# Another opening for layer 1 of a two-layer decoder trunk: transposed x, sums over features, and other placements

## The chip, the core and the metric

The kernel runs on one core of one Trainium2 chip. The metric is the device time of one execution in microseconds; the median of several runs counts. The profile is one execution recorded by the hardware profiler. TensorE multiplies, VectorE and ScalarE do the elementwise work, GpSimd (POOL) little, and SyncE (SP) issues nearly all DMAs.

## What is computed

Two layers on x (512 tokens x 2048 features, float32). Each layer normalises x, modulates it by a conditioning vector c, mixes tokens and adds the gated result:

```python
c_act = jax.nn.silu(c)
for i in range(2):
    mod = (c_act @ ada_w[i] + ada_b[i])[:, None, :]
    shift, scale, gate = jnp.split(mod, 3, axis=-1)
    h = rmsnorm(x, norm_g[i]) * (1.0 + scale) + shift
    y = retention_branch(h, ...) if i == 0 else mla_branch(h, ...)
    x = x + gate * y
return rmsnorm(x, final_norm_g)
```

`retention_branch` begins with `proj = h @ w_in`, where `w_in` holds the columns of q, k, v and a gate g for eight heads. The change concerns only what comes before and beside the first head's part of that product.

## The kernel before, in words

All work on h is done transposed: features on the 128 partitions, the 512 tokens along the free axis. The 2048 features are 16 blocks `kt` of 128, and two blocks make a pair `u` (8 pairs). For each block the kernel needs hT[kt] = a * xT + b, where xT is x transposed and multiplied by each token's 1/rms, and the columns a and b come from the conditioning. Matrices are split into a high part (float32r) and a low part (the rest), and every product is three matmuls: high by high and the two mixed ones.

The conditioning columns are dot products of rows of `ada_w`, transposed on the host (`ada_t`), with silu(c). `load_mod` loads 128 such rows (`aw`, 1 MiB, four buffers; in halves of 512 KB for blocks 0 and 1), and `sum_mod` forms the sums on VectorE with one SCALAR_TENSOR_TENSOR that multiplies and adds up, for a whole block or per half. After the second half a VectorE add joins both. `make_shift` and `make_first` (ScalarE) turn the sums into b_col and a_col; `make_first` also writes the high part of hT and a full copy `hf`, from which VectorE makes the low part.

The opening before, in order. SP loads x as eight half tiles of 512 KB (four token tiles of 128 x 2048 in two halves), then the first `aw`, then weights and more `aw` in turn. c (one row) is spread over all partitions by four one-row float32 matmuls (c_ps), and ScalarE takes the silu. Per token tile `square` sums the squares along the free axis, one half tile on ScalarE and the other on VectorE; GpSimd raises the mean to the power -1/2. `diagonal` puts the factor on a 128x128 diagonal, and `transpose` multiplies blocks of x by it on TensorE, which transposes and normalises at once. This is done for blocks 0 to 5; ScalarE copies them from PSUM to SBUF (`keep_x`). The matmuls x_r spread the factors over all partitions; `factors` is their copy. For pairs u = 3 to 7 the host's transposed x (`x_t`) is loaded later, in `load_unit`, and `normalise(u)` multiplies it by the factors on VectorE.

Then come the products of the first head: v and g of block 0, v and g of block 1, qk of blocks 0 and 1, and from there pair by pair (`products`, 12 matmuls of 512 columns for one block and one kind, four PSUM banks; `swap` changes banks between v and qk). `prepare_ahead(u)` holds the weight casts, the sums, `normalise` and `make_first` of pair u in the written order. Several things set the order around the change: every instruction wrapped in `queued` is issued behind the last one written so far for ScalarE, VectorE, TensorE and SP, so each engine works in the order of the text; SP issues loads in that order, and a load whose buffer is still in use holds up those behind it. PSUM has four `acc` and four `aux` banks.

Of the kernel before, what the change touches and what calls it, by code (L numbers as in the profile page):

```python
# [49 lines left out]
def hybrid_trunk_kernel(  # L50
# [44 lines left out]
    def big(name, dt=F32R):  # L95
        return base.tile([P, 2, T], dt, tag="big", bufs=16, name=name)
# [16 lines left out]
    def small(name, n=1):  # L113
        return base.tile([P, n], F32, tag="small", bufs=24, name=name)
# [267 lines left out]
    def sum_mod(kt, s, half=None):  # L382

        aw, n = mods[kt, s], 1 if half is None else 2
        if half != 1:
            mod_halves[kt, s] = small(f"mc_{kt}_{s}", n)
        col, j = mod_halves[kt, s], half or 0
        cols = slice(j * D // n, (j + 1) * D // n)
        DVE.scalar_tensor_tensor(  # L389
            out=aw[:, cols], in0=aw[:, cols], scalar=1.0, in1=c_all[:, cols], op0=ALU.mult, op1=ALU.mult,  # L390
            accum_out=col[:, j : j + 1],
        )
        if half == 1:
            both = small(f"mc_{kt}_{s}b")
            DVE.tensor_add(both, col[:, 0:1], col[:, 1:2])
            col = both
        if half != 0:
            mods[kt, s] = col

    def make_shift(kt):  # L400
        k1 = slice(kt, kt + 1)
        ACT.activation(b_col[0][:, k1], mods[kt, 0], AF.Identity, bias=bias_c[0][:, k1])

    def make_first(kt):

        k1 = slice(kt, kt + 1)
        if kt > 0:
            queued(make_shift, kt)
        queued(
            lambda: ACT.activation(  # L410
                a_col[0][:, k1], mods[kt, 1], AF.Identity, bias=bias1[:, k1], scale=norm_c[0][:, k1]
            )
        )
        dst, src = big(f"hT_{kt}"), xT[kt // 2][:, kt % 2, :]
# [94 lines left out]
        return f[:, 0:2, :], f[:, 2:4, :]  # L509


    xs = [[big(f"x_{t}_{j}", F32) for j in range(2)] for t in range(NT)]
    for t in range(NT):
        for j in range(2):
            nc.sync.dma_start(
                xs[t][j], x[t * P : (t + 1) * P, j * 1024 : (j + 1) * 1024].rearrange("p (a b) -> p a b", a=2)
            )
    prepares = {}

    def load_first(kind, u):  # L520
# [2 lines left out]
    def load_mods(kt):  # L523
        for s in range(2):
            mods[kt, s] = queued(load_mod, kt, s)

    load_first("v", 0)
    load_mods(0)
    queued(prepares["v", 0].load, 0)
    load_first("g", 0)  # L530
    prepares["g", 0].load(0)
    load_mods(1)
    for kind in "vg":
        queued(prepares[kind, 0].load, 1)
    load_first("qk", 0)


    c_all = l0p.tile([P, D], F32, name="c_all")
    queued(ACT.dma_start, c_all[0:1, :], c)
    queued(ACT.dma_start, rt, rot_c)  # L540
    queued(ACT.activation, small("silu_first"), ones[:, 0:1], AF.Silu)
    c_ps = [acc(f"c_ps{j}") for j in range(4)]
    for j, ps in enumerate(c_ps):
        queued(PE.matmul, ps, ones[0:1, :], c_all[0:1, j * T : (j + 1) * T], True, True)

    def silu(j):
        ACT.activation(c_all[:, j * T : (j + 1) * T], c_ps[j], AF.Silu)

    bias1 = l0p.tile([P, KD], F32, name="bias1")

    ss = [small(f"x_ss_{t}", 2) for t in range(NT)]
    norm = [None] * NT

    def square(t):
        ACT.activation(k4b(f"x_sq_{t}_0", F32), xs[t][0], AF.Square, accum_out=ss[t][:, 0:1])
        DVE.scalar_tensor_tensor(
            out=k4b(f"x_sq_{t}_1", F32), in0=xs[t][1], scalar=1.0, in1=xs[t][1], op0=ALU.mult, op1=ALU.mult,
            accum_out=ss[t][:, 1:2],
        )
        s1 = small(f"x_s1_{t}")  # L560
        DVE.tensor_add(s1, ss[t][:, 0:1], ss[t][:, 1:2])
        norm[t] = rsqrt(s1, 1, 1.0 / D, f"x_{t}")

    diags = []

    def diagonal(t):
        diags.append(l0p.tile([P, P], F32, tag="diag", bufs=4, name=f"x_diag{t}"))
        if t == NT - 1:
            ACT.activation(diags[t], ident, AF.Identity, scale=norm[t])
        else:  # L570
            DVE.tensor_scalar(out=diags[t], in0=ident, scalar1=norm[t], scalar2=None, op0=ALU.mult)
# [4 lines left out]
    xT = [k4(f"xT_{u}", F32) for u in range(NU)]  # L576
    xT_ps = []

    def transpose(t):

        if t == 0:
            xT_ps.extend(aux(f"xT_ps_{kt}") for kt in range(4))
        for kt in range(4):
            queued(
                PE.matmul, xT_ps[kt][:, t * P : (t + 1) * P],
                xs[t][0][:, kt // 4, (kt % 4) * P : (kt % 4 + 1) * P], diags[t], True, True,
            )

    for t in range(NT):
        queued(square, t)
        queued(silu, t)
        if t == 0:
            queued(
                lambda: DVE.scalar_tensor_tensor(
                    out=bias1, in0=bias_c[0][:, KD:], scalar=1.0, in1=norm_c[0], op0=ALU.add, op1=ALU.mult
                )
            )
        else:  # L600
            queued(diagonal, t - 1)
            transpose(t - 1)
    POOL.dma_start(c_d, c_all[0:1, :])
    queued(sum_mod, 0, 0, 0)
    queued(diagonal, NT - 1)
    transpose(NT - 1)

    def keep_x(kt, ps):
        queued(ACT.copy, xT[kt // 2][:, kt % 2, :], ps)

    for kt in range(3):
        keep_x(kt, xT_ps[kt])
    x_r = aux("x_r")
    for t in range(NT):
        queued(PE.matmul, x_r[:, t * P : (t + 1) * P], ones, diags[t], True, True)
    factors = tmp("x_factors")


    more_ps = [aux(f"xT_ps_{kt}") for kt in (4, 5)]
    for t in range(NT):  # L620
        for kt, ps in zip((4, 5), more_ps):
            queued(
                PE.matmul, ps[:, t * P : (t + 1) * P], xs[t][0][:, kt // 4, (kt % 4) * P : (kt % 4 + 1) * P], diags[t],
                True, True,
            )

    def normalise(u):
        DVE.tensor_mul(xT[u], xT[u], factors.unsqueeze(1).to_broadcast([P, 2, T]))
# [1 line left out]
    def load_unit(u):  # L630
        here, there = ("v", "qk") if u % 2 == 0 else ("qk", "v")
        if u > 1:
            load_first(here, u)
        load_mods(2 * u)
        if u == 1:
            load_first(here, u)
        if u > 2:
            queued(nc.sync.dma_start, xT[u], x_t[u])
# [14 lines left out]
    def prepare_ahead(u, first=None, between=lambda: None):  # L653
# [6 lines left out]
        queued(sum_mod, 2 * u, 0)  # L660
        if first is not None and u > 2:
            queued(first)
        if u > 2:
            queued(normalise, u)
        queued(low)
        queued(sum_mod, 2 * u, 1)
# [45 lines left out]
    queued(low)  # L712
    queued(low_qk)
    queued(sum_mod, 2, 0, 0)
    queued(products, "v", 1)
    queued(products, "g", 1)
    queued(swap, "v", "qk")
# [13 lines left out]
    for u in range(1, NU):  # L731
# [1884 lines left out]
```

## Time and profile before

| | |
|---|---|
| time, median of 3 runs | 2119.43 us (2119.42 to 2119.93) |
| profiled execution, first to last instruction | 2118.4 us |
| TensorE busy | 2104.0 us (99%) |
| VectorE, ScalarE, GpSimd busy | 1676.0, 1055.5, 103.6 us |
| DMA | 462.95 MB, 219 GB/s in the mean |

Times in the rows below are microseconds from the first instruction, unless ns is written. A matmul of float32 operands appears as two passes (two MATMUL records); one of float32r operands as a single one. PE is TensorE's matmul side, PEld its loading of weights.

### The profile page before, as it was taken

How to read it: one execution, taken by the hardware profiler on the slowest of the kernel's cores; microseconds unless marked ns; L12 is line 12 of the kernel's file. 1: busy time of each engine (PE TensorE's matmuls, PEld its weight loads, DVE VectorE, ACT ScalarE, POOL GpSimd, SP SyncE). 2: the span in 40 equal slices, each digit the busy share in tenths (PEclk: the TensorE clock that was granted, in tenths of full speed). 3: DMA queues.
4: the chain of work that ended last, by engine and by line, in shares of the span. 5: the costliest groups of instructions: out<-in, count | busy, mean ns of one | idle time of the engine just before them, and what ended most of it. 6: DMA issues, size and time to landing. Idle time of an engine off the chain costs nothing.

```text
span 2118.4 us, 30062 instructions
## 1 busy us (share of the span) xinstructions
PE 2104.0 (99%) x11124; PEld 1812.6 (86%) x11124; DVE 1676.0 (79%) x2506; ACT 1055.5 (50%) x1622; POOL 103.6 (5%) x176
## 2 busy tenths in 40 slices
PE   8999999999999999999999999999999999999998
PEld 6888898989889888888888888898889989888888
DVE  7899888888888789666777778768978788886665
ACT  6765444444454444434344444345446575664443
POOL 1001010000000000000000000010001000000000
PEclk9999999999999999999999999999999999999999
DMA  9975786868787778856657556753566644346643
GB/s 381 406 280 195 248 276 222 283 211 272 239 263 250 242 229 283 265 172 196 222 173 241 201 198 230 258 191 108 164 189 209 190 129 149 118 137 219 222 142 138
DMA packets 230101, 462.95 MB, mean 219 GB/s; under 512 B 20881, under 2 KB 84401, under 8 KB 226369
## 3 DMA queue, kind: packets, MB, share of 16 engines
q1 hardware_dynamic: 217312, 421.07, 60.3%
q0 software_dynamic: 11920, 38.91, 4.7%
q8 instruction: 87, 1.43, 0.3%
q10 hardware_dynamic: 722, 1.06, 0.2%
q14 instruction: 60, 0.49, 0.1%
HBM read 417.96 MB, written 43.00 MB: 218 GB/s over the span
## 4 chain that ended last, share of the span: by engine, by line
PE 96%; DMA 1%; DVE 1%; ACT 0%; issue 0%; SPq 0%; DVEq 0%
PE o L1486 16%; PE o L2450 4%; PE x L884 2%; PE x L883 2%; PE x L885 2%; PE y L885 2%; PE y L884 2%; PE s L885 2%; PE s L884 2%; PE s L883 2%; PE y L883 2%; PE uv L2046 2%; PE qk L158 2%; PE s_qk L984 2%; PE x_qk L984 2%; PE qk L160 2%
## 5 line engine op out<-in xcount | busy, mean ns | idle before, releaser
L1486 PE MATMUL o<-o_h,o_p 128*128 128x512 f32 (+1 forms) x1088 | 323.0, 378 | 0.0
L1486 PEld LDWEIGHTS o<-o_h,o_p 128*128 128x128 f32 x1088 | 200.2, 188 | 37.1
L1486 PE MATMUL o<-o_l,o_p 128*128 128x512 f32 (+1 forms) x544 | 204.8, 376 | 0.0
L136 DVE TENSOR_TENSOR o_p<-o_r,o_p 128x1024 fp32r<-128x1024 f32 x64 | 78.1, 1222 | 54.3 <-ACT o_p L135 54.1
L1486 PEld LDWEIGHTS o<-o_l,o_p 128*128 128x128 f32 x544 | 102.3, 188 | 18.3
L2450 PE MATMUL o<-o_h,o_w 128*128 128x512 f32 (+1 forms) x336 | 82.7, 337 | 0.0
L1170 DVE SCALAR_TENSOR_TENSOR mod<-mod,c_odd 128x1024 f32<-128x1024 f32 x56 | 67.2, 1219 | 15.3 <-DMA mod<-in_ada_t_dram 15.3
L135 ACT CAST o_p<-o_r 128x1024 fp32r<-128x1024 f32 x64 | 66.7, 1054 | 22.4 <-PE o L1486 13.3
L158 PE MATMUL qk<-hT,qk_p 128*128 128x512 f32 x192 | 75.0, 391 | 0.0
L160 PE MATMUL qk<-hT,qk_p 128*128 128x512 f32 x192 | 74.9, 390 | 0.0
L389 DVE SCALAR_TENSOR_TENSOR aw<-aw,c_all 128x2048 f32<-128x2048 f32 (+1 forms) x37 | 73.2, 1997 | 2.1 <-DMA aw<-in_ada_t_dram 2.1
L159 PE MATMUL qk<-hT,qk_p 128*128 128x512 f32 x192 | 74.7, 389 | 0.0
L2450 PEld LDWEIGHTS o<-o_h,o_w 128*128 128x128 f32 x336 | 57.7, 188 | 6.9
L2450 PE MATMUL o<-o_l,o_w 128*128 128x512 f32 (+1 forms) x168 | 56.5, 337 | 0.0
L136 DVE TENSOR_TENSOR o_l<-o_in,o_h 128x1024 fp32r<-128x1024 f32 x24 | 29.3, 1222 | 34.2 <-ACT o_h L135 34.2
L1332 ACT ACTIVATE yn<-y,nmr,gn_r 128x512 f32<-128x512 f32 x32 | 22.3, 778 | 67.7 <-DVE nmr L1326 67.7
L135 ACT CAST o_h<-o_in 128x1024 fp32r<-128x1024 f32 x24 | 25.3, 1052 | 61.6 <-PE o L159 40.5
L158 PE MATMUL o<-o_h,o_w 128*128 128x512 f32 x128 | 50.1, 391 | 0.0
L160 PE MATMUL o<-o_h,o_w 128*128 128x512 f32 x128 | 49.8, 389 | 0.0
L159 PE MATMUL o<-o_l,o_w 128*128 128x512 f32 x128 | 49.8, 389 | 0.0
L1170 DVE SCALAR_TENSOR_TENSOR mod<-mod,c_bm 128x1024 f32<-128x1024 f32 x40 | 48.7, 1219 | 0.0
L448 PE MATMUL g<-hT,g_p 128*128 128x512 f32 x192 | 46.1, 389 | 0.0
(1532 smaller groups left out, 6238.3 us busy)
## 6 DMA issues: line engine op xcount, KB each, us to landing
mod<-in_ada_t_dram SPq DMA_DIRECT2D x96, 512.0 KB, 5.7
o_r<-in_ret_w_out_dram SPq DMA_DIRECT2D x64, 512.0 KB, 5.5
aw<-in_ada_t_dram SPq DMA_DIRECT2D x28, 1024.0 KB, 9.5
mod_gate<-in_ada_t_dram SPq DMA_DIRECT2D x32, 512.0 KB, 4.4
o_w_raw<-in_mla_w_out_dram SPq DMA_DIRECT2D x32, 512.0 KB, 4.4
qk_r<-in_ret_w_in_dram SPq DMA_DIRECT2D x48, 256.0 KB, 3.5
qk_r<-qk_d SPq DMA_DIRECT2D x32, 256.0 KB, 6.1
v_r<-v_d SPq DMA_DIRECT2D x32, 256.0 KB, 5.7
```

The lines of the kernel that those rows point to most:

```text
L135: ACT.copy(hi, src)
L136: DVE.tensor_sub(lo, src, hi.bitcast(F32))
L158: PE.matmul(o, lhs[0], rhs[0], start=first and not seeded, stop=False, skip_group_check=seeded)
L159: PE.matmul(o, lhs[0], rhs[1], start=False, stop=False, skip_group_check=seeded)
L160: return PE.matmul(o, lhs[1], rhs[0], start=False, stop=last, skip_group_check=seeded)
L883: PE.matmul(banks[b], a[0], w[0], start=first, stop=False, skip_group_check=True)
L884: PE.matmul(banks[b], a[0], w[1], start=False, stop=False, skip_group_check=True)
L885: PE.matmul(banks[b], a[1], w[0], start=False, stop=True, skip_group_check=True)
L984: PE.matmul(o, w[wp][:, i, b * P : (b + 1) * P], a[ap], start=first and i + b + k == 0, stop=k == 2, skip_group_check=True,)
L1170: DVE.scalar_tensor_tensor(out=aw, in0=aw, scalar=1.0, in1=silu_c[j], op0=ALU.mult, op1=ALU.mult, accum_out=row_sums[piece][:, j, b : b + 1],)
L1486: PE.matmul(o, w[i][:, ki, c0 + b * P : c0 + (b + 1) * P], a[j], start=first and i + j == 0, stop=last and i == 1, skip_group_check=True,)
L2450: PE.matmul(banks2[b][:, cols], w[0][i][:, 0, b * P : (b + 1) * P], o2_moving(w, u, cols)[j], start=u + i + j == 0, stop=u == KD - 1 and i ...
```

## The change

In words: the x read at the start is now mostly the host's transposed x. SP loads pairs 2 to 7 of `x_t` first (six times 512 KB), then the first half of `aw` for block 0, then the first 512 features of the four token tiles (four times 256 KB), then `vecs` (bias and gain columns, before on GpSimd's queue), then the rest in turn. Pairs 0 and 1 are still transposed on TensorE, all four token tiles in one place, and x_r with them. The squares of pairs 2 to 7 are formed on ScalarE and added up elementwise on VectorE (`square_pair`); TensorE sums them over the partitions (`x_sums`), and the squares of the first 512 features are summed on ScalarE as before (`square`, `norm_pair`). The diagonals are all made on ScalarE. The row c is split into a high and a low float32r part (`row_parts`) and spread by eight one-row matmuls (`row_spread`). Six matmuls whose result nobody reads (`keep_busy`) are put between. hT_0 is formed straight from PSUM and in two halves, and ScalarE copies the factors before a_col. The two half sums are joined on ScalarE: the first half goes into the bias (`half_shift`, `half_scale`), the second is added to it. Pair 2 is normalised on VectorE like the later ones, the loads of `x_t` leave `load_unit`, and the load of `rot` and the store `c_d` move.

```diff
-    POOL.dma_start(vcol, vecs)
...
-        if half == 1:
-            both = small(f"mc_{kt}_{s}b")
-            DVE.tensor_add(both, col[:, 0:1], col[:, 1:2])
-            col = both
         if half != 0:
-            mods[kt, s] = col
+            mods[kt, s] = col[:, n - 1 : n]
+
+    def half_shift(kt):
+        k1 = slice(kt, kt + 1)
+        ACT.activation(b_col[0][:, k1], mod_halves[kt, 0][:, 0:1], AF.Identity, bias=bias_c[0][:, k1])
+
+    def half_scale(kt):
+        k1 = slice(kt, kt + 1)
+        ACT.activation(
+            bias1[:, k1], mod_halves[kt, 1][:, 0:1], AF.Identity, bias=bias1[:, k1], scale=norm_c[0][:, k1]
+        )
...
-        dst, src = big(f"hT_{kt}"), xT[kt // 2][:, kt % 2, :]
+        dst, src = big(f"hT_{kt}"), xT[kt // 2][:, kt % 2, :] if kt > 0 else xT_ps[0]
-        n = 2 if kt == 1 else 1
+        n = 2 if kt < 2 else 1
...
+    queued(ACT.dma_start, c_all[0:1, :], c)
+    for u in range(2, NU):
+        nc.sync.dma_start(xT[u], x_t[u])
...
+    queued(load_mod_half, 0, 0)
+    for t in range(NT):
+        nc.sync.dma_start(xs[t], x[t * P : (t + 1) * P, 0:T])
+    nc.sync.dma_start(vcol, vecs)
     load_first("v", 0)
-    load_mods(0)
+    queued(load_mod_half, 0, 1)
+    queued(load_mod_half, 1, 0)
     queued(prepares["v", 0].load, 0)
+    queued(load_mod_half, 1, 1)
...
+    def row_parts(j):
+        cols = slice(j * 1024, (j + 1) * 1024)
+        queued(ACT.copy, c_row[0][j], c_all[0:1, cols])
+        queued(DVE.tensor_sub, c_row[1][j], c_all[0:1, cols], c_row[0][j].bitcast(F32))
+
+    def row_spread(j):
+        for i in range(2):
+            queued(PE.matmul, c_ps[j], one_row, c_row[i][j // 2][:, j % 2 * T : (j % 2 + 1) * T], i == 0, i == 1)
...
+    def keep_busy(src):
+        queued(PE.matmul, early, ones, src, True, True)
...
+    def square_pair(u):
+        sq = sq_sum if u == 2 else k4b(f"x_sq_{u}", F32)
+        queued(ACT.activation, sq, xT[u], AF.Square)
+        if u == NU - 1:
+            queued(DVE.tensor_add, sq_sum[:, 0, :], sq_sum[:, 0, :], sq_sum[:, 1, :])
+            for i in range(2):
+                queued(DVE.tensor_add, sq_sum[:, 0, :], sq_sum[:, 0, :], sq[:, i, :])
+        elif u > 2:
+            queued(DVE.tensor_add, sq_sum, sq_sum, sq)
...
+    row_parts(0)
+    square_pair(2)
+    row_parts(1)
+    square_pair(3)
+    keep_busy(xT[2][:, 0, :])
+    keep_busy(xT[2][:, 1, :])
+    row_spread(0)
+    row_spread(1)
+    silu(0)
+    square_pair(4)
+    silu(1)
+    keep_busy(xT[4][:, 0, :])
+    row_spread(2)
+    row_spread(3)
+    square_pair(5)
+    silu(2)
+    square_pair(6)
+    silu(3)
+    keep_busy(xT[6][:, 0, :])
+    square_pair(7)
+    queued(sum_mod, 0, 0, 0)
+    x_sums = acc("x_sums")
+    for t in range(NT):
+        queued(PE.matmul, x_sums[:, t : t + 1], sq_sum[:, 0, t * P : (t + 1) * P], crow, True, True)
...
     for t in range(NT):
         queued(square, t)
...
+    for t in (2, 3):
+        keep_busy(xs[t])
+    norm_pair(0)
+    norm_pair(2)
...
+    for t in range(NT):
+        diagonal(t)
+        cols = slice(t * P, (t + 1) * P)
+        for kt in range(4):
+            queued(PE.matmul, xT_ps[kt][:, cols], xs[t][:, kt * P : (kt + 1) * P], diags[t], True, True)
+        queued(PE.matmul, x_r[:, cols], ones, diags[t], True, True)
...
-        if u > 2:
+        if u > 1:
             queued(normalise, u)
...
+    queued(half_shift, 0)
     queued(sum_mod, 0, 0, 1)
     queued(make_shift, 0)
+    queued(sum_mod, 0, 1, 0)
+    queued(half_scale, 0)
     low_v = queued(prepares["v", 0], 0)
-    for half in range(2):
-        queued(sum_mod, 0, 1, half)
+    queued(ACT.copy, factors, x_r)
+    queued(sum_mod, 0, 1, 1)
     low = make_first(0)
     queued(low_v)
     queued(sum_mod, 1, 0, 0)
     low_g = queued(prepares["g", 0], 0)
     queued(low)
     queued(low_g)
-    keep_x(3, xT_ps[3])
-    queued(ACT.copy, factors, x_r)
-    for i, ps in enumerate(more_ps):
-        keep_x(4 + i, ps)
+    for kt in range(1, 4):
+        keep_x(kt, xT_ps[kt])
+    queued(nc.sync.dma_start, c_d, c_all[0:1, :])
+    queued(half_shift, 1)
     queued(sum_mod, 1, 0, 1)
...
-    for half in range(2):
-        queued(sum_mod, 1, 1, half)
+    queued(sum_mod, 1, 1, 0)
+    queued(half_scale, 1)
+    queued(sum_mod, 1, 1, 1)
     lows = [queued(prepares[kind, 0], 1) for kind in "vg"]
...
+        if u == 2:
+            queued(ACT.dma_start, rt, rot_c)
```

## Rows read from the trace of the kernel before

**Rows 1.** The page: span, and busy time with its share and instructions.
```profile
span 2118.4 us, 30062 instructions
PE 2104.0 (99%) x11124; PEld 1812.6 (86%) x11124; DVE 1676.0 (79%) x2506; ACT 1055.5 (50%) x1622; POOL 103.6 (5%) x176
```
**Rows 2.** Waits of TensorE, whole span: engine, line, waited for: total us, times, longest.
```profile
PE c_ps L474 <- DMA c_all<-in_c_dram: 3.2, 1, 3.2
PE xT_ps L474 <- DVE x_diag L571: 2.2, 3, 1.2
PE v L448 <- DVE hT L423: 0.9, 1, 0.9
```
**Rows 3.** Chain of waits, first 120 us: start, duration, what ended last.
```profile
52.31 10.61 DMA aw<-in_ada_t_dram
...
63.02 2.30 DVE aw L389 x2
...
65.98 1.19 PE v L448 x4
...
69.91 8.16 PE qk L448 x36
```
**Rows 4.** Timeline of TensorE: start, duration, line, out<-in, form, passes, [idle before].
```profile
3.25 7.16 PE L474 MATMUL c_ps<-c_all,ones 1*128 1x512 f32 x8 [3.25 <-DMA c_all<-in_c_dram]
...
16.79 4.07 PE L474 MATMUL xT_ps<-x_diag,x 128*128 128x128 f32 x16 [0.48 <-DVE x_diag L571]
20.65 1.92 PE L474 MATMUL x_r<-x_diag,ones 128*128 128x128 f32 x8
22.36 2.04 PE L474 MATMUL xT_ps<-x_diag,x 128*128 128x128 f32 x16
24.16 3.00 PE L448 MATMUL v<-pair,hT 128*128 128x512 f32 x12
...
29.98 3.12 PE L448 MATMUL v<-pair,hT 128*128 128x512 f32 x12
```
**Rows 5.** Timeline of ScalarE, the same columns.
```profile
4.72 1.06 ACT L555 ACTIVATE x_sq<-x 128x1024 f32<-128x1024 f32 x1 [1.52 <-DMA x<-in_x_dram]
...
22.91 0.80 ACT L422 ACTIVATE h_0f<-xT,b_col,a_col 128x512 f32<-128x512 f32 x1
...
24.61 0.58 ACT L474 COPY x_factors<-x_r 128x512 f32<-128x512 f32 x1
...
28.90 0.39 ACT L410 ACTIVATE a_col<-mc_1b,bias,vcol 128x1 f32<-128x1 f32 x1 [0.26 <-DVE mc_1b L395]
29.32 1.10 ACT L420 ACTIVATE hT<-xT,b_col,a_col 128x256 fp32r<-128x256 f32 x2
...
55.92 1.04 ACT L361 CAST g_p<-g_raw 128x1024 fp32r<-128x1024 f32 x1
56.87 1.04 ACT L361 CAST qk_p<-qk_raw 128x1024 fp32r<-128x1024 f32 x1
```
**Rows 6.** Timeline of VectorE, the same columns.
```profile
14.85 1.23 DVE L556 SCALAR_TENSOR_TENSOR x_sq<-x 128x1024 f32<-128x1024 f32 x1 [0.68 <-DMA x<-in_x_dram]
...
23.75 0.69 DVE L423 TENSOR_TENSOR hT<-h_0f,hT 128x512 fp32r<-128x512 f32 x1
...
27.44 1.22 DVE L389 SCALAR_TENSOR_TENSOR aw<-aw,c_all 128x1024 f32<-128x1024 f32 x1
```
**Rows 7.** One line's instructions, L2483: durations min/median/max in ns, first and last start.
```profile
L2483 PE MATMUL x_sums<-ones,x_sq x8: 250/250/271, 2106.2 to 2107.3; 128*128 128x1 f32 x8
```
**Rows 8.** Windows: stretch, its length, busy by engine, granted clock, DMA share, GB/s.
```profile
6.00:7.00 1.00, 1.00 (x3) 0.48 (x2) 0.99 (x1) 0.35 (x1) 0.00 (x0) 1.00 0.99 231
...
8.00:9.00 1.00, 1.00 (x2) 0.33 (x1) 0.18 (x1) 0.52 (x1) 0.38 (x1) 1.00 1.01 414
```
**Rows 9.** Windows at the end of the span, the same columns.
```profile
2111.00:2112.00 1.00, 0.13 (x2) 0.00 (x0) 1.00 (x2) 0.67 (x1) 0.00 (x0) 1.00 1.04 381
...
2115.00:2116.00 1.00, 0.00 (x0) 0.00 (x0) 0.00 (x0) 0.00 (x0) 0.00 (x0) 0.50 1.03 258
```

More of the change, by code (lines that the diff above doesn't have):

```diff
@@ L509, in staged0 @@
         return f[:, 0:2, :], f[:, 2:4, :]
[L512 to L517, printed above, removed]
+    xT = [k4(f"xT_{u}", F32) for u in range(NU)]
+    xs = [base.tile([P, T], F32, tag="big", bufs=16, name=f"x_{t}") for t in range(NT)]
     prepares = {}
@@ L525, in load_mods, with load_mod_half @@
             mods[kt, s] = queued(load_mod, kt, s)
+    c_all = l0p.tile([P, D], F32, name="c_all")
+    c_row = [
+        [base.tile([1, 1024], F32R, tag="big", bufs=16, name=f"c_row{i}{j}") for j in range(2)] for i in range(2)
+    ]
+    queued(ACT.dma_start, c_all[0:1, :], c)
+    for u in range(2, NU):
+        nc.sync.dma_start(xT[u], x_t[u])
+    mods[0, 0], mods[0, 1] = (l0p.tile([P, D], F32, tag="aw", bufs=4, name=f"aw_0_{s}") for s in range(2))
+    def load_mod_half(s, j):
+        cols = slice(j * 1024, (j + 1) * 1024)
+        nc.sync.dma_start(mods[0, s][:, cols], ada_t[0, s * D : s * D + P, cols])
+    queued(load_mod_half, 0, 0)
+    for t in range(NT):
+        nc.sync.dma_start(xs[t], x[t * P : (t + 1) * P, 0:T])
+    nc.sync.dma_start(vcol, vecs)
     load_first("v", 0)
-    load_mods(0)
+    queued(load_mod_half, 0, 1)
+    queued(load_mod_half, 1, 0)
     queued(prepares["v", 0].load, 0)
+    queued(load_mod_half, 1, 1)
     load_first("g", 0)
-    prepares["g", 0].load(0)
+    queued(prepares["g", 0].load, 0)
     load_mods(1)
@@ L535, in hybrid_trunk_kernel @@
     load_first("qk", 0)
-    c_all = l0p.tile([P, D], F32, name="c_all")
-    queued(ACT.dma_start, c_all[0:1, :], c)
-    queued(ACT.dma_start, rt, rot_c)
     queued(ACT.activation, small("silu_first"), ones[:, 0:1], AF.Silu)
     c_ps = [acc(f"c_ps{j}") for j in range(4)]
-    for j, ps in enumerate(c_ps):
-        queued(PE.matmul, ps, ones[0:1, :], c_all[0:1, j * T : (j + 1) * T], True, True)
+    one_row = base.tile([1, P], F32R, tag="tmp", bufs=6, name="one_row")
+    DVE.tensor_copy(one_row, ones[0:1, :])
@@ L546, in silu @@
+    def row_parts(j):
+        cols = slice(j * 1024, (j + 1) * 1024)
+        queued(ACT.copy, c_row[0][j], c_all[0:1, cols])
[3 more added lines that the diff above has]
+            queued(PE.matmul, c_ps[j], one_row, c_row[i][j // 2][:, j % 2 * T : (j % 2 + 1) * T], i == 0, i == 1)
     def silu(j):
-        ACT.activation(c_all[:, j * T : (j + 1) * T], c_ps[j], AF.Silu)
+        queued(ACT.activation, c_all[:, j * T : (j + 1) * T], c_ps[j], AF.Silu)
@@ L549, in hybrid_trunk_kernel @@
     bias1 = l0p.tile([P, KD], F32, name="bias1")
-    ss = [small(f"x_ss_{t}", 2) for t in range(NT)]
-    norm = [None] * NT
-    def square(t):
[L555 to L558, printed above, removed]
-        )
-        s1 = small(f"x_s1_{t}")
-        DVE.tensor_add(s1, ss[t][:, 0:1], ss[t][:, 1:2])
-        norm[t] = rsqrt(s1, 1, 1.0 / D, f"x_{t}")
@@ L564, in hybrid_trunk_kernel @@
-    diags = []
+    early = aux("early")
+    def keep_busy(src):
+        queued(PE.matmul, early, ones, src, True, True)
+    sq_sum = k4b("x_sq_2", F32)
+    def square_pair(u):
[7 more added lines that the diff above has]
+            queued(DVE.tensor_add, sq_sum, sq_sum, sq)
@@ new lines, in hybrid_trunk_kernel, with norm_pair @@
+    ss = [small(f"x_ss_{i}", NT) for i in range(4)]
+    norm = small("x_norm", NT)
+    def square(t):
+        queued(lambda: ACT.activation(tmp(f"x_sq_{t}"), xs[t], AF.Square, accum_out=ss[0][:, t : t + 1]))
+    def norm_pair(t):
+        two = slice(t, t + 2)
+        queued(
+            lambda: DVE.scalar_tensor_tensor(
+                out=ss[2][:, two], in0=ss[0][:, two], scalar=1.0 / D, in1=ss[1][:, two], op0=ALU.mult, op1=ALU.add
+            )
+        )
+        queued(lambda: POOL.tensor_tensor(out=norm[:, two], in0=ss[2][:, two], in1=mhalf[:, 0:2], op=ALU.pow))
@@ L566, in diagonal @@
+    diags = [l0p.tile([P, P], F32, tag="diag", bufs=4, name=f"x_diag{t}") for t in range(NT)]
     def diagonal(t):
[L567 to L571, printed above, removed]
+        queued(lambda: ACT.activation(diags[t], ident, AF.Identity, scale=norm[:, t : t + 1]))
@@ L575, in hybrid_trunk_kernel @@
     tables = rotary_tables(*ret_tables, 0, False, "ret", ACT)
[L576 to L587, printed above, removed]
+    row_parts(0)
+    square_pair(2)
+    row_parts(1)
@@ L591, in hybrid_trunk_kernel @@
+    queued(
+        lambda: DVE.tensor_scalar(
+            out=ss[1], in0=x_sums[:, 0:NT], scalar1=1.0 / D, scalar2=EPS, op0=ALU.mult, op1=ALU.add
+        )
+    )
     for t in range(NT):
         queued(square, t)
[L593 to L606, printed above, removed]
+    for t in (2, 3):
+        keep_busy(xs[t])
+    norm_pair(0)
+    norm_pair(2)
+    queued(
+        lambda: DVE.scalar_tensor_tensor(
+            out=bias1, in0=bias_c[0][:, KD:], scalar=1.0, in1=norm_c[0], op0=ALU.add, op1=ALU.mult
+        )
+    )
+    x_r = acc("x_r")
+    xT_ps = [aux(f"xT_ps_{kt}") for kt in range(4)]
+    for t in range(NT):
[4 more added lines that the diff above has]
+        queued(PE.matmul, x_r[:, cols], ones, diags[t], True, True)
@@ L608, in keep_x @@
+    factors = tmp("x_factors")
     def keep_x(kt, ps):
         queued(ACT.copy, xT[kt // 2][:, kt % 2, :], ps)
[L611 to L625, printed above, removed]
@@ L636, in load_unit @@
             load_first(here, u)
-        if u > 2:
-            queued(nc.sync.dma_start, xT[u], x_t[u])
         if u > 1:
@@ L662, in prepare_ahead @@
             queued(first)
-        if u > 2:
+        if u > 1:
             queued(normalise, u)
@@ L714, in hybrid_trunk_kernel @@
     queued(sum_mod, 2, 0, 0)
+    queued(half_shift, 2)
     queued(products, "v", 1)
```

3 lines of the change are left out of this document (2 added, 1 removed).

## Prediction

> **What bounds the kernel now.** I read the page first, then who waited for whom on TensorE, then the chain of waits of the first 120 us, then the first 60 us engine by engine. TensorE is busy for 2104.0 us of a span of 2118.4 us [rows 1], so time can only come from places where it idles or multiplies nothing useful. The view of waits puts nearly all idle time into the opening: 3.2 us before the first matmul, 2.2 us between groups of transposes, and one wait of 0.9 us for the low part of hT [rows 2]. After 65.98 us TensorE runs on without a gap that counts, 36 matmuls of 512 columns in 8.16 us, 0.2267 us each [rows 3]. So the question is: **when can the matmuls at 65.98 us start after the change?** Everything behind them moves along.
>
> The chain shows what holds them. The load of `aw` for feature block 6 lands at 62.9, VectorE sums it for 2.3 us, then makes the low part of hT_5, and only then does TensorE go on [rows 3]. The first 62 us are thus partly a matter of DMA, which runs at some 410 GB/s from 8 us on [rows 8]. TensorE alone would have been there sooner: from the second feature block's products at 29.98 [rows 4] to the matmuls at 65.98 there are 152 matmuls, 34.5 us at 0.2267, which gives 64.4. So 1.5 us of the 36.0 are stalls; about 1.0 of it is the wait on that load, 0.5 are short waits for hT. If the front comes up to 1 us late, the wait for `aw` absorbs it; if it comes early, that wait grows, because the same 4 MiB of x are still loaded ahead of it.
>
> The clock: the granted clock reads 1.00 in every early row, but the pace is that of 1.2 GHz. Eight passes of c_ps took 7.16 us, 0.895 each, and sixteen of the transposes 3.86 us, 0.24 each, up to 20.65; the sixteen that start at 22.36 need 1.80 us up to the first product, 0.11 each, the pace of 2.4 GHz [rows 4]. Before it rose, TensorE had worked without a gap from 16.79 on; 7.16 us of one-row matmuls had not raised it.
>
> **The change, part by part.** *Loads.* Before the first product, x costs 4 MiB as before (six transposed pairs 3 MiB, four quarter rows 1 MiB). The 2.5 MiB saved are those of pairs 3 to 7 behind 54 us, where TensorE and not DMA is late: worth nothing. The table `rot` and `vecs` leave the start; at 6 to 7 us the DMA moved 231 GB/s against 414 at 8 to 9 us [rows 8], so up to 1 us of load time may come back, less what `vecs` costs on SP. On SP, `vecs` and later the copy `c_d` wait for nothing that is late; the moved load of `rot` costs ScalarE one DMA issue at u = 2, beside a full TensorE.
>
> *ScalarE up to the last squares.* The first pair can be there at 4.72, as the first half tile of x was [rows 5]. ScalarE then does six squares and the second row copy; such instructions of 1024 columns take 1.06 and follow each other after 0.95 [rows 5], so 6.7 us. The four silus add 0.5 each, 2.0. It also waits for TensorE, which has to do two `keep_busy` first: each is two passes of 512 columns, at 0.895 [rows 4] 3.6 us for the two, to 8.3; then one-row matmuls, and c_ps0 is ready at about 9.2, when ScalarE has been idle since 7.6. A shorter wait of this kind comes before silu 2 (0.6). Sum: 4.7 + 6.7 + 2.0 + 1.6 + 0.6 = 15.6 for the last pair square. The data are there: the last 512 KB of x landed at 14.85 [rows 6], and half a MiB of `aw` is now ahead of the quarter rows.
>
> *Sum of squares and factors.* VectorE adds as ScalarE delivers; behind the last square stand two adds of 512 columns, 0.69 each [rows 6], as long as the low part of hT, so 17.1. TensorE sums across partitions in eight passes; the one similar group took 1.35 us for eight at the high clock [rows 7], I take 1.8 at the low one: 19.0. The roots (VectorE, POOL, ScalarE) need another 2 us, to about 21.5, but TensorE does two more `keep_busy` first: 3.6 us at the low pace, to 22.6. So these hide the roots and cost 1 us on top.
>
> *Transposes.* What was spread over the time up to 24.16, tile by tile, now comes in one block: 16 transposes and 4 of x_r, 40 passes. The two ends are 0.24 and 0.11 each [rows 4], 9.4 or 4.4 us. I take the high pace: by then TensorE has worked without a gap since 17.1. So x_r is done at E = 27.0.
>
> At this place the trace has to be weighed against what the early `keep_busy` are for. TensorE's last matmul ended just after 2111 and the granted clock was at 0.50, the 1.2 GHz level, in 2115 to 2116 [rows 9]: idle time of a few us brings it back. In the opening TensorE would stand idle from about 11 or 15 us to 17.1. If the clock rises with the first tiles and holds, the sums, `keep_busy` and transposes are 3 us shorter (rival 1); I hold it likelier that it is low at 17. The Trainium skill, "TensorE: Matmul & The Clock Gate", section "HAM oscillation", says that a kernel whose bursts of matmuls are parted by waits for data falls back to the low clock and pays for the rise each time. By that rule the early `keep_busy` gain nothing and the forecast stands; without it rival 1 would.
>
> *First products.* The new order on ScalarE puts the copy of x_r (`factors`) ahead of a_col and hT_0, so hT_0 waits for the very last of the 40 passes; before it needed only block 0. From E: 0.3 to drain (estimate from the 250 ns of a one-column pass [rows 7]), `factors` 0.58, a_col 0.42 until the next begins, hT_0 in two halves 1.0, its full copy 0.80 [rows 5]: E + 3.1 = 30.1. Before, that copy ended at 23.71. TensorE's first products can start at E + 1.9, but the next block's decide: behind the full copy VectorE has, in order, the low parts of hT_0 and g and three half sums of 1.22 [rows 6], then come a_col and hT_1. That took 6.3 us before (23.71 to 29.98). The two joining adds go (0.3 less), but `half_scale` now stands on ScalarE ahead of the casts of v and g and waits for the second of these sums (0.3 more): 6.3 again. The second block's products start at 36.4 instead of 29.98: **6.4 us late**. VectorE's idle time in between, over 5 us, can't be used, as the low part of hT_0 is queued ahead of the sums.
>
> *What is given back.* The wait for `aw` at 63 us vanishes (1.0). VectorE gets one multiplication of 1024 columns (1.22 [rows 6]) at u = 2, as pair 2 now has to be normalised; it fits into 2 us of waits for loads that vanish too, and may cost 0.1 to 0.2 of TensorE. `aw` of block 3 is issued some 6 us later, as its buffers come free with those sums; its users are late by the same. So 6.4 - 0.9 = 5.5.
>
> **Rivals.** *1. The clock is up from the first tiles and holds.* Then ScalarE waits less (last square at 14.6), the sums end at 17.6, two `keep_busy` take 1.7, 40 passes 4.4: E = 23.8, 3.2 earlier. For it: two `keep_busy` are 3.6 us of full matmuls at the start. Against it: one-row matmuls behind them, which didn't raise it before, and the idle stretch ahead of the sums. 2119.4 + 2.3 = 2121.7.
>
> *2. Faster: the opening is bound by loads alone.* If hT_0's full copy came by 23.7 despite the block of passes, only the load of `aw` at 62.9 would decide, and the quieter start of the DMA would bring it about 1 us forward: 2118.4. The point is E = 20.6 for the copy, and 21.5 for no change at all; that needs the chain to the last square to be over 3 us shorter than worked out, at the high clock. Little speaks for it: the 0.95 per square and 0.11 per pass are read, not guessed. That the reading of x only moves, and saves nothing where it matters, is in this rival's and in the forecast's sum alike.
>
> *3. Later still.* The clock stays low for the 40 passes as well (E up to 31.9), or the later issue of `aw` makes DMA run dry. Each would add 3 to 5 us: 2128 to 2130.
>
> **How the numbers follow.** The sums are differences inside the profiled execution (span 2118.4), whose median run took 2119.43, 1.0 more around the span; I carry the difference over. Forecast: 2119.4 + 5.5 = 2124.9, chance 0.50, with its own spread 2123.0 to 2127.0 from where the clock rises and from ScalarE's queue. Rival 1: 0.28, at 2121.7, from 2120.8 on. Rival 2: 0.11. Rival 3: 0.11. The range 2120.8 to 2127.0 leaves out rivals 2 and 3. A difference of 0.2%, 4.2 us, is about what can be told from no change. Slower by more than that: most of the forecast (0.42), rival 3 (0.11), a little of rival 1 (0.02), 0.55. Within: 0.08 + 0.26 + 0.10 = 0.44. Faster by 4.2 us would need all of the opening's gaps: 0.01.
>
> **What would show it.** In the profile after: c_ps done past 9 us, the last pair square near 15.6, `x_sums` near 17 to 19, transposes in one block from 22.6 at 0.11 a pass, `factors` at 27.3, the second block's v products near 36, VectorE idle for some us ahead of hT_0's low part, and no gap at 66 us. Transposes done by 24 show rival 1; the first hT_0 ahead of 22 us shows rival 2. It would be wrong if ScalarE and VectorE did not run in the order written, or if the pace of the passes were another.

## The result, and the profile after

The changed kernel took 2125.64 us in the median of eight runs (2124.41 to 2126.81), the kernel before, run beside it, 2119.89 us (2118.85 to 2120.45). The ratio is 1.0026 with a 95% interval of 1.0017 to 1.0036: 5.75 us slower, where 5.5 had been forecast. The profiled execution took 2126.18 us, its span is 2124.4 us against 2118.4 before.

The page, for [rows 1]:

```profile
span 2124.4 us, 30076 instructions
PE 2106.9 (99%) x11128; PEld 1811.5 (85%) x11128; DVE 1679.5 (79%) x2496; ACT 1061.6 (50%) x1636; POOL 101.8 (5%) x172
```

TensorE's waits over the whole span, the three largest, for [rows 2] (line, waited for: total us, times, longest):

```profile
PE early L480 <- DMA xT<-in_x_t_dram: 4.6, 1, 4.6
PE v L454 <- ACT hT L426: 3.1, 2, 1.6
PE x_sums L480 <- DVE x_sq L480: 2.4, 1, 2.4
```

TensorE is busy 2.9 us longer, and its three largest waits make 10.1 us instead of 6.3: that is 6.7 us against a span 6.0 us longer. Two kinds of wait are gone, that for the diagonals and that for the low part of hT. Two new ones stand in the list: 1.6 us twice for hT on ScalarE, and 2.4 us for the squares.

The chain of waits shows where the loss ends up, at the four matmuls that were at 65.98 [rows 3]:

```profile
71.67 0.62 DVE hT L429
72.28 0.04 issue
72.33 1.19 PE v L454 x4
...
76.25 8.16 PE qk L454 x36
```

They start at 72.33, 6.35 us later. From the last pass of the opening up to them the chain holds no load any more, only work of VectorE and ScalarE (sums, casts, hT and its low parts). All of the span's 6.0 us, then, has been lost by 72 us. TensorE's timeline, for [rows 4], shows when:

```profile
4.59 3.75 PE L480 MATMUL early<-xT,ones 128*128 128x512 f32 x4 [4.59 <-DMA xT<-in_x_t_dram]
8.27 2.07 PE L480 MATMUL c_ps<-c_row,one_row 1*128 1x512 f32 x4
10.27 2.07 PE L480 MATMUL early<-xT,ones 128*128 128x512 f32 x2
...
14.27 2.08 PE L480 MATMUL early<-xT,ones 128*128 128x512 f32 x2
18.73 1.84 PE L480 MATMUL x_sums<-ones,x_sq 128*128 128x1 f32 x8 [2.38 <-DVE x_sq L480]
20.42 3.64 PE L480 MATMUL early<-x,ones 128*128 128x512 f32 x4
23.90 1.05 PE L480 MATMUL xT_ps<-x_diag,x 128*128 128x128 f32 x8
...
28.14 0.39 PE L480 MATMUL x_r<-x_diag,ones 128*128 128x128 f32 x2
30.09 3.05 PE L454 MATMUL v<-pair,hT 128*128 128x512 f32 x12 [1.56 <-ACT hT L426]
...
37.39 3.12 PE L454 MATMUL v<-pair,hT 128*128 128x512 f32 x12 [1.53 <-ACT hT L426]
```

The second block's products start at 37.39 instead of 29.98, 7.41 late; of this 1.06 comes back up to 72.33. The rest is read on ScalarE and VectorE. ScalarE, for [rows 5]: the two silus that waited, the last pair square, `factors`, and the full copy of hT_0:

```profile
9.52 0.60 ACT L480 ACTIVATE c_all<-c_ps 128x512 f32<-128x512 f32 x1 [2.10 <-PE c_ps L480]
...
13.53 0.60 ACT L480 ACTIVATE c_all<-c_ps 128x512 f32<-128x512 f32 x1 [1.03 <-PE c_ps L480]
...
15.45 1.06 ACT L480 ACTIVATE x_sq<-xT 128x1024 f32<-128x1024 f32 x1
...
28.57 0.59 ACT L480 COPY x_factors<-x_r 128x512 f32<-128x512 f32 x1 [2.52 <-PE x_r L480]
...
30.39 0.78 ACT L428 ACTIVATE h_0f<-xT_ps,b_col,a_col 128x512 f32<-128x512 f32 x1
```

VectorE, for [rows 6]: the adds of the squares, and the low part of hT_0 with the last sum behind it:

```profile
15.10 1.23 DVE L480 TENSOR_TENSOR x_sq<-x_sq,x_sq 128x1024 f32<-128x1024 f32 x1 [1.35 <-ACT x_sq L480]
16.36 0.69 DVE L480 TENSOR_TENSOR x_sq<-x_sq 128x512 f32<-128x512 f32 x1
17.16 1.42 DVE L480 TENSOR_TENSOR x_sq<-x_sq,x_sq 128x512 f32<-128x512 f32 x2
...
31.19 0.69 DVE L429 TENSOR_TENSOR hT<-h_0f,hT 128x512 fp32r<-128x512 f32 x1 [3.27 <-ACT h_0f L428]
...
34.70 1.22 DVE L388 SCALAR_TENSOR_TENSOR aw<-aw,c_all 128x1024 f32<-128x1024 f32 x1
```

VectorE stands idle for 3.27 us ahead of the low part of hT_0, with three sums of 1.22 us queued behind it that need nothing from it.

### The profile page after: what moved, and what is told of

Same layout as the page of the kernel before. It is cut to its first block, busy times and chain, and to the rows that moved or that the text cites. A ratio compares the mean times of both kernels' runs of the same rounds, so it can differ in the third digit from the quotient of the medians.

```text
span 2124.4 us, 30076 instructions
## 1 busy us (share of the span) xinstructions
PE 2106.9 (99%) x11128; PEld 1811.5 (85%) x11128; DVE 1679.5 (79%) x2496; ACT 1061.6 (50%) x1636; POOL 101.8 (5%) x172
## 3 DMA queue, kind: packets, MB, share of 16 engines
q10 hardware_dynamic: 722, 1.06, 0.2%
## 4 chain that ended last, share of the span: by engine, by line
PE 97%; DVE 1%; issue 1%; ACT 1%; DMA 0%; DVEq 0%
PE o L1534 16%; PE o L2498 4%; PE x L932 2%; PE x L933 2%; PE s L933 2%; PE y L933 2%; PE x L931 2%; PE y L932 2%; PE s L932 2%; PE y L931 2%; PE s L931 2%; PE uv L2094 2%; PE qk L158 2%; PE s_qk L1032 2%; PE x_qk L1032 2%; PE qk L160 2%
```

## Experiments

The theory: the loss is made of waits that the written order brings in. The early `keep_busy` delay the squares, `factors` delays hT_0, and hT_0's low part delays the sums of block 1. The rivals: the clock's height decides, or the loads do. Every kernel is compared with the kernel before of the same session. The runs of one kernel spread over 1.4 to 4.1 us, so parts under 1 us are read from the places of the matmuls in the profiled execution. "The end of the front" below is the start of the four matmuls of block 5 that were at 65.98 before and 72.33 after.

### The `keep_busy` matmuls

**no_early_busy**: the first four are left out (nobody reads their result).

```diff
-    keep_busy(xT[2][:, 0, :])
-    keep_busy(xT[2][:, 1, :])
...
-    keep_busy(xT[4][:, 0, :])
...
-    keep_busy(xT[6][:, 0, :])
```

> The first four keep_busy (on pairs 2, 2, 4 and 6) are left out, nothing else. Theory: they only hold up c_ps and with it ScalarE; the last pair square ends near 13.5 instead of 16.5, x_sums starts near 15 instead of 18.7, and the 40 passes still run at the high pace of 0.11, since the last two keep_busy raise the clock. x_r is then done near 24.5 instead of 28.4, the second block's v products start near 33.5 instead of 37.4, and the kernel is 2 to 3 us slower than before, not 6. Rival: the early ones are what raises the clock. Then the 40 passes take 0.24 each, x_r is done at 29 or later and the time stays at before + 6.

Measured: 2123.89 us against 2120.08, 3.8 slower than before instead of 5.75 (ratio 1.0019, 1.0009 to 1.0028), where 2 to 3 had been expected. TensorE's timeline:

```profile
15.51 1.84 PE L480 MATMUL x_sums<-ones,x_sq 128*128 128x1 f32 x8 [5.94 <-DVE x_sq L480]
17.21 3.76 PE L480 MATMUL early<-x,ones 128*128 128x512 f32 x4
20.76 1.75 PE L480 MATMUL xT_ps<-x_diag,x 128*128 128x128 f32 x8
...
22.57 1.06 PE L480 MATMUL xT_ps<-x_diag,x 128*128 128x128 f32 x8
```

The sums start 3.2 us earlier (15.51 for 18.73), because the silus no longer wait for TensorE. The sums and the late `keep_busy` have the same pace as with the early ones (1.84 and 3.76 us). Only the first transposes are slower, 1.75 for eight instead of 1.05, so x_r is done 2.5 earlier, not 3.2. Between these two executions, then, the early `keep_busy` cost 3.2 us and gave 0.7 back; the 0.7 is not sure to be theirs, as in `three`, also without them, the first eight transposes took 1.16. By the medians their net cost is 1.9.

**no_busy**: the two late ones left out as well (`keep_busy(xs[t])` for t = 2 and 3).

> All six keep_busy are left out. Theory (the clock is low unless full matmuls run without a gap just ahead): the 40 passes run at 0.24 at first, 9.4 us if it never rises, and start when the roots are ready, near 19 to 20; x_r done at 28 to 29.5, later than in no_early_busy by 4, time before + 5 to 7. Rival: keep_busy only costs time; then the 40 passes end by 24 and the time is that of before + 1 to 2.

Measured: 2124.56 us, 4.5 slower than before (1.0022, 1.0012 to 1.0031), 0.7 slower than with the late ones, which the spread of the runs doesn't tell from nothing. The transposes start at 19.07 instead of 20.76, but run at 0.23 us a pass until about 24. The second block's products are at 35.28 instead of 34.94. The expectation (5 to 7 slower than before) had the late ones worth more. They shorten the block of passes by 2.0 us (26.42 - 19.07 against 26.08 - 20.76), and they start it 1.7 later: nearly all that their clock gives they cost themselves.

### The order on ScalarE and VectorE

**factors_later**: `factors` behind the full copy of hT_0, all `keep_busy` kept.

```diff
-    queued(ACT.copy, factors, x_r)
     queued(sum_mod, 0, 1, 1)
     low = make_first(0)
+    queued(ACT.copy, factors, x_r)
```

> ScalarE copies x_r (factors) behind hT_0's full copy instead of ahead of a_col. Theory: hT_0 then waits only for block 0's last transposes; v products of block 0 start near 28.5 instead of 30.1, those of block 1 near 35.8 instead of 37.4, time 1.6 us less than the changed kernel, before + 4.2. Rival: something else, the a_col column or VectorE, holds hT_0: no change, before + 5.8.

Measured: 2124.92 us, 4.8 slower than before (1.0022, 1.0013 to 1.0032), 0.9 less than the changed kernel. From the last of the 40 passes to the second block's products it takes 7.5 us (27.78 to 35.29) instead of 8.9, so 1.4 less: hT_0 now needs block 0's transposes alone. This execution shows something else too, on TensorE's timeline and in the windows (stretch, length, busy by engine with TensorE first, granted clock, DMA share, GB/s):

```profile
7.86 1.19 PE L480 MATMUL c_ps<-c_row,one_row 1*128 1x512 f32 x4
8.98 1.12 PE L480 MATMUL early<-xT,ones 128*128 128x512 f32 x2
...
11.39 2.08 PE L480 MATMUL early<-xT,ones 128*128 128x512 f32 x2
...
18.38 3.76 PE L480 MATMUL early<-x,ones 128*128 128x512 f32 x4
```

```profile
10.00:11.00 1.00, 1.00 (x5) 0.66 (x4) 0.80 (x1) 1.00 (x3) 0.00 (x0) 0.91 1.06 434
11.00:12.00 1.00, 1.00 (x3) 0.50 (x2) 0.79 (x2) 1.00 (x3) 0.00 (x0) 0.50 0.98 399
```

Here the early `keep_busy` did raise the clock: from 8 us on a `keep_busy` of two passes takes 1.12 us instead of 2.07. At about 10.8, among the one-row matmuls and with TensorE busy throughout, the granted clock falls to 0.50, and the fourth `keep_busy`, the sums and the late ones go at the low pace again. So whether or not these four raise the clock early, it is low at 16 to 22 us in both executions.

The mean granted clock, on record for every run, shows how often this happens. It is 0.996 in this execution and 0.999 in the profiled one of the changed kernel. Of the changed kernel's eight runs four have 0.996 or 0.997 and are 4.9 us slower than before in the mean; four have 0.999 and are 6.4 slower. `factors_later` and `sums_first` have four runs of ten at 0.996 or 0.997; no kernel without the four `keep_busy` in these places has a run below 0.998. So in some two of five executions they seem to raise the clock for a while, which is worth 1.5 to 2.3 us. That the clock rose and fell in those runs as it did here is read from the mean alone. Among the runs at 0.999 and above, `no_early_busy` is 2.6 us faster than the changed kernel, `factors_later` 1.1 and `sums_first` 1.4.

**sums_first**: the four half sums of block 1 ahead of hT_0's low part on VectorE.

```diff
-    queued(sum_mod, 1, 0, 0)
+    for s_ in range(2):
+        for half in range(2):
+            queued(sum_mod, 1, s_, half)
     low_g = queued(prepares["g", 0], 0)
     queued(low)
...
-    queued(sum_mod, 1, 0, 1)
...
-    queued(sum_mod, 1, 1, 0)
...
-    queued(sum_mod, 1, 1, 1)
```

> VectorE does all four half sums of block 1 before the low part of hT_0, in the time in which it sat idle (24.6 to 26.1 and 27.9 to 31.2). Theory (the order of VectorE's queue is what delays block 1): its v products start near 36.0, bound by ScalarE then, instead of 37.4; the gap of 1.5 us on TensorE behind block 0's products nearly closes; time 1.4 us less than the changed kernel, before + 4.4. Rival: ScalarE's own queue (copies of pairs 0 and 1, casts) is the bound anyway: block 1 at 37.4, before + 5.8.

Measured: 2124.67 us, 4.6 slower than before (1.0020, 1.0010 to 1.0029), 1.2 less than the changed kernel. TensorE's timeline:

```profile
33.31 2.89 PE L454 MATMUL g<-hT,g_p 128*128 128x512 f32 x12
36.04 2.90 PE L454 MATMUL v<-pair,hT 128*128 128x512 f32 x12
```

The second block's products follow g without a gap; the second wait of 1.53 us for hT is gone. It was the order on VectorE that had made this wait.

**three**: the first four `keep_busy` out, `factors` later and the sums first, together.

> The three edits so far in one kernel: first four keep_busy left out, factors behind hT_0's full copy, the four half sums of block 1 ahead of hT_0's low part. Theory (each takes a different piece off one chain: the last square, hT_0's wait, VectorE's idle time): v products of block 0 start near 25.5 to 26, those of block 1 near 31.3 with no gap between, TensorE gapless to the end, the matmuls that stand at 72.3 in the changed kernel at 66.3 to 66.8, time before + 0.3 to + 1.0. Rival: the pieces overlap and their gains don't add up: before + 2.5 or more.

Measured: 2121.31 us against 2119.90, 1.4 slower (1.0006, 0.9997 to 1.0015). The three single gains, 1.9, 0.9 and 1.2, sum to 4.0; together they gave 4.3. The front ends at 68.0. That is still a little more than expected, because of a new wait:

```profile
29.65 1.20 PE L454 MATMUL v<-pair,hT 128*128 128x512 f32 x4 [1.15 <-DVE hT L429]
```

Now hT_0 is early, and its low part stands behind the sums that were put ahead of it.

**three_xr**: besides, the x_r passes behind all the transposes, as hT_0 and not x_r is now waited for.

> As three, and the matmuls of x_r come behind all sixteen transposes instead of one behind each token tile. Theory: they fill TensorE's wait for hT_0; block 0's products start 0.6 us earlier than in three, time before - 0.3 to + 0.4. Rival: loads of aw bound the front by then as they do before, and a wait of some tenths shows near 66 us; time as three.

Measured: 2121.08 us, 1.2 slower (1.0006, 0.9997 to 1.0015). In the profile the second block's products start at 32.47 instead of 33.42; the median moved 0.2, which the spread of the runs doesn't tell from nothing. The wait for the low part is still there (1.23 us), and the time is above what was expected.

**mid**: besides, the fourth of these sums behind the low parts.

```diff
-    for s_ in range(2):
-        for half in range(2):
-            queued(sum_mod, 1, s_, half)
+    for s_, half in ((0, 0), (0, 1), (1, 0)):
+        queued(sum_mod, 1, s_, half)
...
     queued(half_scale, 1)
+    queued(sum_mod, 1, 1, 1)
```

> As three_xr, but the last of the four half sums of block 1 stands behind the low parts of hT_0 and g. Theory: TensorE's wait of 1.2 us for the low part of hT_0 (block 0) goes down to some 0.2, block 1's products at 31.1 to 31.5 instead of 32.5, time 1.0 less than three_xr: that of before, +- 0.4. Rival: ScalarE's half_scale or a_col holds block 1: as three_xr, before + 1.2.

Measured: 2120.11 us against 2120.08 (1.0001, 0.9992 to 1.0009): the kernel before is reached. TensorE's timeline, and the chain, in which the front's four matmuls are the last of these twelve:

```profile
27.80 1.21 PE L454 MATMUL v<-pair,hT 128*128 128x512 f32 x4 [0.32 <-DVE hT L429]
...
31.60 2.88 PE L454 MATMUL v<-pair,hT 128*128 128x512 f32 x12
```

```profile
64.41 2.75 PE v L454 x12
```

The wait shrinks to 0.3, the second block's products are at 31.60, and the front ends at 66.2, against 65.98 before. As far as the runs can tell (some 2 us to either side), the whole loss is thus made good by the places of `factors`, x_r and the half sums in the written order and by leaving out four matmuls that nobody reads. The block of passes itself still ends later than the transposes did before, and more sums stand ahead of the low part than before; so part of what these edits win makes up for a loss that they did not cause.

### Whether the clock decides

**fill_only**: the changed kernel, with the four early `keep_busy` moved: on pairs 3 and 4, in one block behind the last one-row matmul, where TensorE would be idle and no silu waits for them.

```diff
-    keep_busy(xT[2][:, 0, :])
-    keep_busy(xT[2][:, 1, :])
...
-    keep_busy(xT[4][:, 0, :])
     row_spread(2)
     row_spread(3)
+    keep_busy(xT[3][:, 0, :])
+    keep_busy(xT[3][:, 1, :])
+    keep_busy(xT[4][:, 0, :])
+    keep_busy(xT[4][:, 1, :])
...
-    keep_busy(xT[6][:, 0, :])
```

> The changed kernel with the four early keep_busy moved: they stand behind the last one-row matmul (on both halves of pairs 3 and 4) and fill the time in which TensorE waits for x_sq, where they hold up nothing. Theory (the clock falls in that idle stretch, and full matmuls right up to x_sums keep it up): x_sums take about 1.0 instead of 1.8, the last two keep_busy 1.7 instead of 3.6, the 40 passes 0.11 each from the first one; the roots (near 20.5) are the bound then and x_r is done near 22.5 to 23, against 25.9 in no_early_busy; v products of block 1 near 32, time before + 1.0 to + 1.8. Rival: the clock isn't up at 15.5 after 6 us of such matmuls either; then as no_early_busy, before + 3.8.

Measured: 2121.27 us, 1.2 slower than before (1.0006, 0.9997 to 1.0015). TensorE's timeline:

```profile
9.54 6.60 PE L480 MATMUL early<-xT,ones 128*128 128x512 f32 x8
16.37 1.02 PE L480 MATMUL x_sums<-ones,x_sq 128*128 128x1 f32 x8 [0.24 <-DVE x_sq L480]
17.26 1.96 PE L480 MATMUL early<-x,ones 128*128 128x512 f32 x4
```

Here the clock is up when the squares are there: the sums take 1.02 instead of 1.84, the late ones 1.96 instead of 3.76. Against no_early_busy this is 2.6 us by the medians, and the second block's products start 2.2 earlier (32.73 for 34.94): what a clock that holds is worth. It is the same means as in the change, put where it delays nobody and isn't followed by idle time.

**filled**: mid and this block of `keep_busy` together.

> mid and fill_only in one. Theory: x_r done near 22 and hT_0 at 22.5; from there VectorE's sums and the loads of aw for block 1 (landing near 26) hold block 1, near 29.5 to 30, and the load of aw for block 6 near 63 holds the front as in the kernel before: time before - 0.8 to + 0.3, and no further gain can come from the opening. Rival: TensorE alone is the bound all the way, and the 2 to 3 us from the clock come through in full: before - 2.

Measured: 2120.62 us, 0.5 slower than before (1.0004, 0.9995 to 1.0012): no better than mid and a little above what was expected (0.8 faster to 0.3 slower), although the same block had brought 2.6 in fill_only. TensorE's timeline, a load in the chain of waits, VectorE's third sum of block 1, and two windows:

```profile
23.26 2.34 PE L454 MATMUL v<-pair,hT 128*128 128x512 f32 x8
27.29 1.90 PE L454 MATMUL v<-pair,hT 128*128 128x512 f32 x4 [1.70 <-DVE hT L429]
28.99 3.83 PE L454 MATMUL g<-hT,g_p 128*128 128x512 f32 x12
```

```profile
16.46 8.91 DMA aw<-in_ada_t_dram
```

```profile
25.40 1.23 DVE L388 SCALAR_TENSOR_TENSOR aw<-aw,c_all 128x1024 f32<-128x1024 f32 x1
```

```profile
22.00:24.00 2.00, 1.97 (x14) 1.69 (x14) 1.89 (x5) 1.74 (x4) 0.00 (x0) 1.00 1.04 414
...
25.00:30.00 5.00, 3.31 (x9) 2.29 (x10) 4.94 (x10) 4.58 (x11) 0.00 (x0) 0.75 1.07 398
```

The first products start at 23.26, 0.9 earlier than before. But hT_0's low part stands behind VectorE's third sum of block 1, and that starts only at 25.40, as its `aw` lands, right behind the second sum. VectorE's waits for loads ahead of it make 1.0 us in all, at a DMA rate of 414 GB/s; the order has its share in TensorE's wait of 1.7 us too, as this sum (1.23) stands ahead of the low part. After it TensorE is still 0.5 us ahead of mid (27.29 for 27.80). Then the clock costs more than that: it falls around the wait (0.75 in the mean of 25 to 30), and four matmuls take 1.90 for 1.21, the next 12 take 3.83 for 2.91. So the second block starts at 32.66, 1.1 later than in mid. A version with this sum elsewhere was not tried, so whether the two gains can be had together stays open. None of these kernels beats the kernel before by more than the runs can tell.

### The start of the loads

**before_quiet**: the kernel before, with `vecs` on SP behind x, `rot` at u = 2, and `bias1` formed later, as it needs `vecs`.

```diff
-    POOL.dma_start(vcol, vecs)
...
+    nc.sync.dma_start(vcol, vecs)
...
-    queued(ACT.dma_start, rt, rot_c)
...
+        if u == 2:
+            queued(ACT.dma_start, rt, rot_c)
```

> The kernel before, with only two loads moved as the change moves them: vecs goes to SP behind the x loads, rot to the pass u = 2 (the bias1 instruction stands behind the first pair of half sums, as vecs is later). Theory of rival 2 in the prediction (the quieter start of DMA brings the loads forward by up to 1 us, and the load of aw for block 6 holds the front): last x tile near 13.8 instead of 14.85, aw of block 6 about 0.8 earlier, time before - 0.6 to - 1.0. Rival: the slow stretch at 6 to 7 us is not due to these two loads: no change.

Measured: 2119.79 us against 2119.90 (1.0000, 0.9992 to 1.0009): nothing. The windows, for [rows 8]:

```profile
5.00:6.00 1.00, 1.00 (x3) 0.48 (x2) 0.13 (x1) 1.00 (x3) 0.00 (x0) 1.00 0.92 160
6.00:7.00 1.00, 1.00 (x2) 0.39 (x2) 1.00 (x1) 0.25 (x1) 0.00 (x0) 1.00 0.63 225
```

The slow stretch stays without the small loads; `before_quiet_join`, also without them, has 225 GB/s in 6 to 7 us as well. Rival 2's gain from a quiet start has fallen.

**before_quiet_join**: besides, the half sums joined on ScalarE as in the change.

> As before_quiet, and the half sums joined on ScalarE as in the change (half_shift, half_scale), nothing else of it. Theory: VectorE loses four small adds of 0.16 ahead of block 1, whose products start 0.3 to 0.6 earlier, but the load of aw for block 6 holds the front anyway: time as before_quiet, within 0.3. Rival: half_scale on ScalarE waits ahead of the casts of v and g and block 1 comes later: up to + 0.5 over before_quiet.

Measured: 2120.23 us (1.0002, 0.9993 to 1.0011). The joins can't be told from nothing, as the prediction had it: less work on VectorE, one more wait on ScalarE.

## Why the prediction was right, and where its sizes were off

**The question was the right one.** All of the loss lies ahead of 72 us; the time went with the start of the matmuls at 65.98.

**The squares on ScalarE: 15.6 forecast, 16.5 measured.** The start (4.47), the pace of 0.95 and the two `keep_busy` (3.75 for 3.6) were as worked out. The waits of the silus were 2.10 and 1.03, for 1.6 and 0.6 in the sum. Ahead of the second lies the third `keep_busy` (2.07 us), between the two halves of the row; the sum gave the 0.6 without a working and named only the first two.

**The adds on VectorE: 1.5 us forecast from the last square to the sums, 2.2 measured.** The sum counted the two adds behind the last square. But the add of pair 6 (1.23) and the fold of the two halves (0.69) end only at 17.05, 0.5 behind that square, and the two wait for them. With the first point the sums start at 18.73 instead of 17.1: this was the largest error.

**Sums, late `keep_busy`, passes.** 1.84 for 1.8, 3.64 for 3.6, 40 passes in 4.63 (23.90 to 28.53) for 4.4. The roots took longer than the 2 us taken: the two powers on GpSimd alone take 2.91 us. The late `keep_busy` hid it, as the prediction said; the last pass ended at 28.5 for 27.0. (At the low pace the 40 passes would make 9.6 us, not the 9.4 of the prediction; only rival 3 uses it.)

**The first products: E + 3.1 forecast, E + 2.6 measured; then 6.3 forecast, 6.2 measured.** The reading that the block of passes, `factors` and the fixed order of VectorE set the second block's start is what factors_later, sums_first and mid show: each place undone gives its part back. The second block is 7.4 late, for 6.4 forecast.

**Given back: 0.9 forecast, 1.06 measured.** The wait of 0.9 us for the low part of hT, which ended behind `aw` [rows 2, 3], has vanished, and TensorE is without a gap from 37.39 to the end of the front but for some 0.4 us (34.94 us for 152 matmuls, 34.5 at 0.2267).

**The total.** By places in the trace it is 6.35, by spans 6.0, by medians 5.75; the forecast of 5.5 is 0.9 below the first and 0.25 below the last. In the terms of the sum the last pass is 1.5 late, the copies 0.5 early, the return 0.2 larger: the errors cancel in part. That the median came within 0.25 is luck. It lies between two groups of runs, 4.9 and 6.4 slower than before (see `factors_later`); the sum takes the low clock up to the passes, as the profiled execution has it, and so belongs beside the 6.4.

**Rival 1**, that the clock rises early and holds, was half right: in the profiled execution of factors_later it rose, and by the mean clock in half of the changed kernel's runs, and it did not hold. In the Trainium skill's "TensorE: Matmul & The Clock Gate", section "HAM oscillation", bursts parted by waits fall back to the low clock. The trace of filled agrees: around a wait of 1.70 us the granted clock fell. The fall in factors_later is another case, as TensorE was busy in it (1.00 of 1.00 us) with one-row matmuls. fill_only shows the 2.6 us that a burst without a pause gives. **Rival 2** needed the full copy of hT_0 by 23.7; it ended at 31.17. Its gain fell with before_quiet, and filled shows what else stands against it: with hT_0 earlier than before, the loads of `aw` for block 1 come in beside the order of the sums. Of **rival 3**, one half came true without its price: DMA did run dry. SP issued no load between 36.8 and 46.4, as a load of v weights waited 9.0 us for its buffer and `aw` stood behind it; before, DMA moved 406 GB/s in this window. TensorE worked on beside it:

```profile
40.00:50.00 10.00, 10.00 (x46) 8.28 (x45) 10.00 (x12) 7.36 (x13) 0.00 (x0) 1.00 0.55 206
```

## What to carry to other kernels

Matmuls that only keep the clock up belong where TensorE would stand idle up to the work that needs it. Ahead of a matmul that another engine waits for, they lengthen that wait (3.2 us lost for 7.9 us of such matmuls here); and with idle time behind them, the clock was low when the work came (1.84 us for the sums, against 1.02 behind a block without a pause). Where a step is regrouped into one block, its consumers take over the end of the block; so look up, for each instruction in the fixed order of the engines, what is queued behind it that needs less than it does. Price every producer's tail: how far the adding engine is behind when the last piece arrives, not only what is left after that piece.

## What was not expected of the hardware

**Powers on GpSimd.** Before, three of the four powers of 128x1 took 0.55 to 0.58 us, the fourth 1.66. After, two of 128x2 took 2.91 together:

```profile
21.11 2.91 POOL L606 TENSOR_TENSOR x_norm<-x_ss,few 128x2 f32<-128x2 f32 x2 [19.44 <-DVE x_ss L602]
```

The long ones run beside VectorE's sums, which here start at 21.10, 22.24 and 23.38 without a pause; the fourth power before began at 16.63, a sum at 16.65. In fill_only VectorE's sum starts only at 18.25: the power that began at 17.95 took 0.71, the next, beside the sum, 1.40. But a power of 128x2 in the kernel before, at 1430 us, took 0.72 beside a VectorE instruction, so what decides is open.

**The rate of the first loads varies between executions.** In 5 to 6 and 6 to 7 us the profiles of the change's order of loads show 360 and 393 GB/s (the changed kernel), 328 and 418 (sums_first), and 205 and 258 (factors_later). With the order of before, 6 to 7 us had 231, 225 and 225 in its three profiles, with the two small loads or without. What slows an execution there is open.

**The granted clock.** Its record reads 1.00 from the start of the span while passes of 512 columns take 0.90 us and more; only after its first change (factors_later) do record and pace agree. Early on the pace decides.
